# A two-block layer on one core: the gate tiles, the attention inputs and the convolution of the second block in another order

## The chip, the cores and the metric

The kernel runs on one NeuronCore of a Trainium2 chip. The metric is the time on the device in microseconds (us) for one execution, as a median over runs of the same program. Five engines with queues of their own take part: TensorE (PE in the rows, with its weight loads as PEld), VectorE (DVE), ScalarE (ACT), GpSimd (POOL), and SyncE (SP), which here only issues DMAs. Each engine works its queue in order: an instruction that waits holds up all that stands behind it on that engine.

## The reference, cut to what matters

`reference(...)` is a first block (a gated linear recurrence with a Fourier branch and expert-choice experts) and then `second_block`. Only the first half of the second block is touched here. With 512 tokens, 1024 channels, 8 heads of 64 and a convolution over 31 tokens it computes:

```python
proj = rmsnorm_2(x, norm_mix_g) @ w_in           # -> u_glu (1024), q, k, v (512 each), f_logit (8), gate_c, gate_a (1024 each)
a, gate = split(u_glu);  u = a * sigmoid(gate)   # 512 channels
u = causal_depthwise_conv(u, dw_w, 31 taps) + dw_b
conv_out = silu(layernorm(u, ln_g, ln_b)) @ pw_w            # -> 1024
c = cumsum(log_sigmoid(f_logit + fox_bf))                   # per head
s = (q @ k.T) * 64**-0.5 + c[query] - c[key]                # causal mask, softmax
attn_out = (softmax(s) @ v) @ attn_branch_w                 # -> 1024
merged = sigmoid(gate_c) * conv_out + sigmoid(gate_a) * attn_out
x = x + merged @ w_out                                      # then cross attention, experts, last norm
```

## The kernel before, in words

Every float32 matrix product is made of products of two parts: an operand is split into H (its rounded first part) and L (the rest), and three products (H·H, H·L, L·H) are summed; that is `mm3`, lines 87 to 90. A weight half of 128 rows by 512 comes from HBM as part of a 1 MB `raw` tile, ACT writes its H (`wH`, line 128) and GpSimd, or in places VectorE, its L (`wL`, line 129); four such pairs fit in the pool `wpc`. A projection tile of 128 output columns over 512 tokens (`ws_tile`) takes two halves, so 24 products; a tile with 512 input channels takes one half and 12 products. The `raw` tiles lie in four slots in this phase, and their loads stand in SP's queue.

The function touched is `phase_c`. Before the change it puts its work out in this order. The two norms between the blocks give the transposed input `hx` and write the normed rows back into `xres`, the residual (line 1246). Then come the gated linear unit, as two tiles of gates, two of values, and again (lines 1252 to 1263); the depthwise convolution on VectorE, 31 instructions for each of four channel tiles, from padded inputs `upad` into `cacc` (lines 1267 to 1277); the forget gates `fc` (lines 1281 to 1302); eight tiles of queries and keys and the values (lines 1305 to 1314); the layer norm over the channels with its `mean` and `var` products on TensorE (lines 1330 to 1354); and the attention, head by head.

`stack(p)` prepares a pair of heads. For each of the two it copies the first part of queries and keys into one half of the partitions of two tiles and the rest of the queries, and the first part of the keys once more, into the other half (ACT at lines 1370, 1371 and 1374, GpSimd at 1372 and 1373). These tiles take the four slots of the padded inputs: the first head's two tiles take the slots of the first two channel tiles of the convolution, which are free once the convolution has read them. `scores(h)` then makes three products for each of four blocks of queries: first parts with rests (1386), first part with the rest of the keys (1387), and the forget term through a selecting column (1388); the softmax runs on VectorE and ACT (1389 to 1396). `mix` transposes the weights `P`, copies them (`PT`, ACT or VectorE, lines 1408 and 1410), and multiplies with the values. Between two heads stand two steps named in the string `GC`: "G" is a gate tile of the convolution branch (24 products and a tanh), "C" a tile of its output product (12 products). After the last head the function `branch` makes for each of eight tiles the other gate (24 products) and the attention's output product (12).

What stands on a queue, and in which order, is decided by the framework's scheduler: it starts from the order in which the program emits its instructions and from what it thinks each takes, lets an instruction pass others when it believes it ready, and the result is fixed when the program is built. The order can be read without running; `tc.issue_after(i)` keeps what follows behind instruction `i`.

## Time and profile before

| what | value |
|---|---|
| median of 3 runs (lowest, highest) | 1777.76 us (1777.0, 1778.08) |
| span of the profiled execution, first to last instruction | 1772.1 us |
| median less that span | 5.7 us |
| mean granted TensorE clock | 0.969 of full speed |
| PE, PEld busy | 90 %, 59 % of the span |
| DVE, ACT, POOL busy | 49 %, 35 %, 30 % |
| HBM traffic over the span | 216 GB/s |

The profiled execution has no time of its own beside its span; the 5.7 us are what lies around the span, measured on other runs of the same program. Matmuls overlap in the records: one of 512 columns is on record for about 0.39 us and the next starts 0.23 us later, so counts in a window tell more than busy sums.

### The profile page before, as it was taken

What the parts mean: (1) busy time and instruction counts of PE and PEld (TensorE: products, weight loads), DVE (VectorE), ACT (ScalarE), POOL (GpSimd) and SP (SyncE); (2) the same over time, 40 slices, a digit from 0 to 9 for tenths busy, and PEclk for the clock granted to TensorE, in tenths of its full rate; (3) what the DMA queues carried; (4) which work ended last, traced back from release to release, by engine and by line L of the source; (5) the groups of instructions that cost most, each with busy time, mean ns of one, the idle gap of its engine ahead of it and who ended that gap; (6) DMA issues with size and microseconds to landing.
All of it is one profiled execution on the core that took longest, in us unless ns stands there. A gap on an engine that the chain in (4) does not pass through costs nothing. (4 is left out here: it accounts for less than half of the span.)

```text
span 1772.1 us, 20890 instructions
## 1 busy us (share of the span) xinstructions
PE 1597.7 (90%) x7766; PEld 1051.9 (59%) x7766; DVE 876.3 (49%) x1625; ACT 611.6 (35%) x1244; POOL 538.1 (30%) x431
## 2 busy tenths in 40 slices
PE   5988999999999999999999979779999988788884
PEld 4766677777775344434434347656667866666663
DVE  5388554333651221212122057996543264578886
ACT  3433355333430000000000152316533354478883
POOL 2213323344430000000000025745334442456654
PEclk9988999999999999999999989889999999889997
DMA  9423214454768999999999873111022229479934
GB/s 303 156 97 113 99 60 137 148 165 153 255 232 315 386 386 386 386 387 386 386 387 386 326 217 105 47 59 61 25 71 72 98 71 326 150 244 337 324 109 159
DMA packets 236076, 377.03 MB, mean 213 GB/s; under 512 B 16174, under 2 KB 107382, under 8 KB 235964
## 3 DMA queue, kind: packets, MB, share of 16 engines
q1 hardware_dynamic: 231644, 367.44, 58.7%
q0 software_dynamic: 4320, 8.16, 1.3%
q8 instruction: 63, 1.03, 0.2%
q14 instruction: 49, 0.40, 0.1%
HBM read 365.30 MB, written 17.83 MB: 216 GB/s over the span
## 5 line engine op out<-in xcount | busy, mean ns | idle before, releaser
L129 POOL TENSOR_TENSOR wL<-raw,wH 128x512 fp32r<-128x512 f32 x220 | 299.0, 1363 | 412.4 <-ACT wH L128 375.8
L128 ACT ACTIVATE wH<-raw 128x512 fp32r<-128x512 f32 x368 | 226.4, 629 | 276.3 <-PE ps L89 146.5
L1065 PE MATMUL ps<-raw,xT 128*64 128x512 f32 x512 | 228.1, 600 | 0.9 <-DMA raw<-in_w_up_e 0.9
L1066 PE MATMUL ps<-raw,xT 128*64 128x512 f32 x512 | 226.7, 600 | 1.6 <-DMA raw<-in_w_up_e 1.6
L1222 POOL TENSOR_TENSOR xg<-xres,raw 128x512 f32<-128x512 f32 x4 | 5.0, 1269 | 494.0 <-DVE xres L1122 494.0
L1066 PEld LDWEIGHTS ps<-raw,xT 128*64 128x64 f32 x512 | 69.4, 139 | 137.6 <-issue 132.6
L129 DVE TENSOR_TENSOR wL<-raw,wH 128x512 fp32r<-128x512 f32 x148 | 127.4, 906 | 28.5 <-ACT wH L128 26.9
L90 PE MATMUL ps<-raw,wL 128*128 128x512 f32 (+1 forms) x320 | 121.7, 380 | 9.7 <-POOL wL L129 9.7
L88 PE MATMUL ps<-raw,wH 128*128 128x512 f32 (+1 forms) x320 | 121.8, 381 | 0.0
L89 PE MATMUL ps<-raw,wH 128*128 128x512 f32 (+1 forms) x320 | 120.8, 378 | 0.0
L1107 DVE TENSOR_TENSOR hid<-hid,ps 128x512 f32<-128x512 f32 x16 | 11.0, 687 | 214.2 <-PE ps L1066 214.2
L1065 PE MATMUL ps<-raw,hidT 128*64 128x512 f32 x256 | 115.0, 596 | 0.0
L1106 ACT ACTIVATE hid<-ps 128x512 f32<-128x512 f32 x16 | 9.6, 597 | 303.7 <-PE ps L1066 303.7
L1066 PE MATMUL ps<-raw,hidT 128*64 128x512 f32 x256 | 113.5, 596 | 0.7 <-DMA raw<-in_w_down_e 0.7
L1276 DVE SCALAR_TENSOR_TENSOR cacc<-upad,dwc,cacc 128x512 f32<-128x512 f32 x120 | 109.1, 968 | 0.6
L88 PE MATMUL ps<-hx,wH 128*128 128x512 f32 x224 | 91.7, 409 | 3.3 <-ACT wH L128 3.3
L90 PE MATMUL ps<-hx,wL 128*128 128x512 f32 x224 | 90.8, 405 | 2.2 <-POOL wL L129 2.0
L89 PE MATMUL ps<-hx,wH 128*128 128x512 f32 x224 | 90.5, 404 | 0.0
L1826 POOL TENSOR_TENSOR dL<-raw,dH 128x512 fp32r<-128x512 f32 x64 | 82.3, 1307 | 21.8 <-ACT dH L1825 21.4
L1066 PEld LDWEIGHTS ps<-raw,hidT 128*64 128x64 f32 x256 | 33.7, 137 | 72.4 <-issue 69.3
L1065 PEld LDWEIGHTS ps<-raw,xT 128*64 128x64 f32 x512 | 69.3, 138 | 11.0 <-issue 8.9
L90 PEld LDWEIGHTS ps<-raw,wL 128*128 128x128 f32 x320 | 61.1, 191 | 23.5 <-POOL wL L129 10.2
(608 smaller groups left out, 3499.6 us busy)
## 6 DMA issues: line engine op xcount, KB each, us to landing
raw<-in_w_gate_e SPq DMA_DIRECT2D x64, 1024.0 KB
raw<-in_w_up_e SPq DMA_DIRECT2D x64, 1024.0 KB
raw<-in_w_down_e SPq DMA_DIRECT2D x64, 1024.0 KB
raw<-in_w_in SPq DMA_DIRECT2D x34, 1024.0 KB
raw<-in_w_ada SPq DMA_DIRECT2D x24, 1024.0 KB
raw<-in_expert_w_gate SPq DMA_DIRECT2D x32, 512.0 KB
raw<-in_expert_w_up SPq DMA_DIRECT2D x32, 512.0 KB
raw<-in_expert_w_down SPq DMA_DIRECT2D x16, 1024.0 KB
```

The source lines that it names most:

```text
L88: mm(ps, l[0], r[0], start=first, stop=False)
L89: mm(ps, l[0], r[1], start=False, stop=False)
L90: mm(ps, l[1], r[0], start=False, stop=last)
L128: self.nc.scalar.activation(out=H, in_=raw_ap, func=AF.Copy)
L129: (eng or self.lsub).tensor_tensor(out=L, in0=raw_ap, in1=H, op=OP.subtract)
L1065: nc.tensor.matmul(ps[0:64, :], act[:, k, 0:64], rA[:, q, :], start=k == 0, stop=k == 7, tile_position=(0, 0))
L1066: nc.tensor.matmul(ps[64:128, :], act[:, k, 64:128], rB[:, q, :], start=k == 0, stop=k == 7, tile_position=(0, 64))
L1106: AC.activation(out=hid, in_=pg, func=AF.Silu)
L1107: V.tensor_tensor(hid, hid, pu, op=OP.mult)
L1222: (nc.gpsimd, V)[XG[e][t]].tensor_tensor(out=xgs[t][e], in0=xs, in1=gf[:, e * 512:(e + 1) * 512], op=OP.mult)
L1276: V.scalar_tensor_tensor(acc, src, c, acc, op0=OP.mult, op1=OP.add)
L1826: (nc.gpsimd, V)[DL[i]].tensor_tensor(out=L, in0=src, in1=H, op=OP.subtract)
```

## The change

Five things change in `phase_c`. The loads for the gated linear unit are issued in pairs, and gate and value tile of the same channels follow one another, so that the convolution has its first input after two tiles rather than three; `gemm_ws2` takes its two tiles from two loads. The attention's gate (columns 3592 on) is no longer made in `branch`: its eight tiles become steps "A", and their tanh is kept in `xres`, whose rows are written to a DRAM tile `xrd` before and read back after. The layer norm becomes five steps "N". Seven gate tiles "G" now stand ahead of the attention (`FIRST`), and the rest of the steps between the heads (`BETWEEN`). `stack(h)` prepares one head; it also writes `qb` (the first part of the queries, with ones in the other half of the partitions) and `kb` (the rest of the keys, with the forget term in the other half), so that two products make a score and the third falls away; `stack(0)` and `stack(1)` are kept behind the last weight split of the seventh gate tile. Lines of comment are taken out all over the file, which moves the line numbers. The core of the diff:

```diff
-GC = "GGGGGCGCGCGCCCCC"
+FIRST = "GGGGGGG"
+BETWEEN = "NGA", "NNAA", "NNAA", "AC", "AC", "AC", "CC", "CCC"
...
-    def gemm_ws2(self, w, c0, act, evac, ct0=0):
...
+    def gemm_ws2(self, tiles, act):
+
+        W = [[self.wsplit(r[:, kk:kk + 4, q:q + 128], 4, 128, (self.nc.gpsimd, self.nc.vector)[E2[2 * j + kk // 4]]) for kk in (0, 4)]
+             for j, (r, q) in enumerate(tiles)]
         pss = [self.ps() for _ in W]
...
+        xrd = self.drp.tile([512, 1024], F32, name="xrd")
+        for t in range(4):
+            nc.sync.dma_start(out=xrd[t * 128:(t + 1) * 128, :], in_=xres[:, t, :])
+        tha = [xres[:, ct // 2, (ct % 2) * 512:(ct % 2 + 1) * 512] for ct in range(8)]
...
-             self.gemm_ws2(w, 512, hx, ev_gate))
-            self.gemm_ws(w, c2, 256, hx, ev_a, c2 // 128)
-
-        # ---- causal depthwise convolution
+            rg, ra = self.cols_chunk(w, 512 + c2, 8, 256), self.cols_chunk(w, c2, 8, 256)
+            for q in (0, 128):
+                ct = (c2 + q) // 128
+                pg, pa_ = (self.gemm_ws2([(rg, 0), (ra, 0)], hx) if ct == 0 else
+                           (self.ws_tile(rg, q, hx, 8), self.ws_tile(ra, q, hx, 8)))
+                ev_gate(ct, pg)
+                ev_a(ct, pa_)
+
...
+        def gate_steps(c0, new):
             for cc in range(0, 1024, 256):
-                r = self.cols_chunk(w, 2568 + cc, 8, 256)
+                r = self.cols_chunk(w, c0 + cc, 8, 256)
                 for q in (0, 128):
                     ct = (cc + q) // 128
...
+        def norm_steps():
+            ps = self.pa(name="mean")
+            for ct in range(4):
+                nc.tensor.matmul(ps, on, xc[ct], start=ct == 0, stop=ct == 3)
...
-                stacks[2 * p + a] = qa, ka, kl
+        def stack(h):
+
+            p, a = divmod(h, 2)
+            q, k = qk[p], qk[4 + p]
+            o, x = slice(64 * a, 64 * a + 64), slice(64 - 64 * a, 128 - 64 * a)
+            qb, kb = qb2[a], kb2[a]
+            qa, ka = (sa.tile([128, 544], F32, tag="upad", name="upad", bufs=NST)[:, 0:512].bitcast(F32R) for _ in range(2))
+            AC.activation(out=qa[o], in_=q[o], func=AF.Copy)
+            AC.activation(out=ka[o], in_=k[o], func=AF.Copy)
+            nc.gpsimd.tensor_tensor(out=qa[x], in0=q[o], in1=qa[o], op=OP.subtract)
+            nc.gpsimd.tensor_tensor(out=kb[o], in0=k[o], in1=ka[o], op=OP.subtract)
+            AC.activation(out=ka[x], in_=ka[o], func=AF.Copy)
+            AC.activation(out=qb[o], in_=q[o], func=AF.Copy)
+            c = x.start + h
+            AC.activation(out=kb[x], in_=cf[x].bitcast(F32), func=AF.Copy, scale=self.selR[x, c:c + 1].bitcast(F32))
+            stacks[h] = qa, ka, qb, kb
 
         def scores(h):
-            """the weights of the keys, queries on the partitions."""
-            qa, ka, kl = stacks.pop(h)
-            r = 64 * (h % 2)
...
                 n = 128 * (i + 1)
                 s = self.pa(name="s")
                 b = slice(i * 128, (i + 1) * 128)
                 nc.tensor.matmul(s[:, 0:n], qa[:, b], ka[:, 0:n], start=True, stop=False)
-                nc.tensor.matmul(s[:, 0:n], qa[r:r + 64, b], kl[r:r + 64, 0:n], start=False, stop=False)
-                nc.tensor.matmul(s[:, 0:n], self.selR[r:r + 40, r + h:r + h + 1].to_broadcast([40, 128]), cf[r:r + 40, 0:n], start=False, stop=True)
+                nc.tensor.matmul(s[:, 0:n], qb[:, b], kb[:, 0:n], start=False, stop=True)
...
+        steps = {"G": gate_steps(2568, new_thc), "A": gate_steps(3592, lambda ct: tha[ct]), "C": conv_steps(), "N": norm_steps()}
+
+        def run(names):
+            for x in names:
+                next(steps[x])
+        run(FIRST)
+        wH, wL = self.split_ins
+        with tc.issue_after(wH), tc.issue_after(wL):
+            stack(0)
+            stack(1)
         nxt = scores(0)
...
             P = nxt
-            if h in (0, 2, 4):
-                stack(h // 2 + 1)
             if h < 7:
                 nxt = scores(h + 1)
-            for x in GC[2 * h:2 * h + 2]:
-                next(gates if x == "G" else convs)
+            if h < 6:
+                stack(h + 2)
+            run(BETWEEN[h])
             if h % 2 == 0:
                 po = self.pa(name="po")
...
+            wr = self.raw(I["attn_branch_w_2"][0][:, cc:cc + 512].rearrange("(k p) c -> p k c", p=128), 4, 512)
+            for c2 in range(0, 512, 128):
+                ct = (cc + c2) // 128
+                py = self.ws_tile(wr, c2, aS, 4)
+                th = tw(name="gth")
+                V.scalar_tensor_tensor(th, tha[ct], 1.0, py, op0=OP.add, op1=OP.mult)
+                V.tensor_tensor(th, thc[ct], th, op=OP.add)
+                H, L = self.split(th, HL("m"), 0.5)
+                mS[0].append(H)
+                mS[1].append(L)
+        for t in range(4):
+            nc.sync.dma_start(out=xres[:, t, :], in_=xrd[t * 128:(t + 1) * 128, :])
+
```

Where instructions move, the order of the queues shows it at three places.

ACT, at the first `stack`, before; `upad` are the stacked heads in the slots of the padded inputs, `qk2` the evacuated queries and keys, `wH` the first parts of weights (the values' weights follow below these rows):

```order
L1309 ACTIVATE qk2_7318<-ps_7285 128x512
L1309 ACTIVATE qk2_7353<-ps_7320 128x512
L1309 ACTIVATE qk2_7390<-ps_7357 128x512
L1370 ACTIVATE upad_7782<-qk2_7318 64x512
L1309 ACTIVATE qk2_7425<-ps_7392 128x512
L128 ACTIVATE wH_7481<-raw_7427 128x512
L1371 ACTIVATE upad_7783<-qk2_7390 64x512
L1374 ACTIVATE upad_7783<-upad_7783 64x512
L128 ACTIVATE wH_7502<-raw_7499 128x512
L128 ACTIVATE wH_7518<-raw_7499 128x512
L1309 ACTIVATE qk2_7462<-ps_7429 128x512
L128 ACTIVATE wH_7537<-raw_7499 128x512
```

ACT, at the first `stack`, after; `thc` are the gates of the convolution branch:

```order
L1333 ACTIVATE thc_7839<-ps_7840 128x512
L129 ACTIVATE wH_7950<-raw_7946 128x512
L129 ACTIVATE wH_7966<-raw_7946 128x512
L1333 ACTIVATE thc_7876<-ps_7877 128x512
L1388 ACTIVATE upad_7983<-qk2_7323 64x512
L1389 ACTIVATE upad_7984<-qk2_7395 64x512
L1393 ACTIVATE qb0_7724<-qk2_7323 64x512
L1392 ACTIVATE upad_7984<-upad_7984 64x512
L1395 ACTIVATE kb0_7726<-fc_7275,selR_229 64x512
L1388 ACTIVATE upad_7992<-qk2_7323 64x512
L1389 ACTIVATE upad_7993<-qk2_7395 64x512
L1393 ACTIVATE qb1_7725<-qk2_7323 64x512
```

The first stack stood among the queries' and keys' projections, ahead of `wH_7502` and of all weight splits behind it; now it stands behind the splits of the seventh gate tile.

PE, at the first score, before; `var` is the norm's variance, `ps` are projection tiles, `s` the scores, `kl` the rest of the keys:

```order
L88 MATMUL ps<-raw,wH 128x512
L1340 MATMUL var<-csq,on_7715 128x512 x4
L1386 MATMUL s<-upad 128x128
L1387 MATMUL s<-kl,upad 128x128
L1388 MATMUL s<-fc,selR 128x128
L1386 MATMUL s<-upad 128x256
L1387 MATMUL s<-kl,upad 128x256
L1388 MATMUL s<-fc,selR 128x256
```

PE, at the norm's `mean`, after; these are the scores of head 1, and `ps` is the eighth gate tile:

```order
L89 MATMUL ps<-raw,wH 128x512
L1406 MATMUL s<-upad 128x384
L1407 MATMUL s<-kb_7727,qb_7725 128x384
L90 MATMUL ps<-raw,wH 128x512
L1406 MATMUL s<-upad 128x512
L1407 MATMUL s<-kb_7727,qb_7725 128x512
L91 MATMUL ps<-raw,wL 128x512
L89 MATMUL ps<-raw,wH 128x512
L1348 MATMUL mean<-cacc,on_7720 128x512 x4
L90 MATMUL ps<-raw,wH 128x512
```

The variance stood right ahead of the first score, seven projection products behind the mean. Now the scores of heads 0 and 1 stand ahead of the mean, seven projection products apart, nine more projection products follow the mean, and then comes the variance; a score has two products where it had three.

DVE, at the norm's reciprocal, before; `crv` is the variance, then its reciprocal root:

```order
L1342 TENSOR_SCALAR crv<-var 128x512
L1389 TENSOR_TENSOR s<-s,mask_n 128x128 x2
L1391 TENSOR_REDUCE am<-s 128x1 x2
L1392 TENSOR_SCALAR am<-am 128x1
L1389 TENSOR_TENSOR s<-s,mask_n 128x128
L1392 TENSOR_SCALAR am<-am 128x1
L1389 TENSOR_TENSOR s<-s,mask_n 128x128
L1391 TENSOR_REDUCE am<-s 128x1
L1344 RECIPROCAL crv<-crv 128x512
L1392 TENSOR_SCALAR am<-am 128x1
L1391 TENSOR_REDUCE am<-s 128x1
L1347 TENSOR_TENSOR cacc<-cacc,crv 128x512 x2
```

DVE, at the same place after; `PT` are the transposed weights of head 0:

```order
L1415 TENSOR_SCALAR P<-P,am 128x512
L1351 TENSOR_TENSOR cacc<-cacc,mean 128x512 x4
L1356 TENSOR_SCALAR crv<-var 128x512
L1358 RECIPROCAL crv<-crv 128x512
L1429 COPY PT<-pt 128x512
L1361 TENSOR_TENSOR cacc<-cacc,crv 128x512 x2
L1362 TENSOR_SCALAR cacc<-cacc,cols_889 128x512 x2
L1429 COPY PT<-pt 128x256
L1361 TENSOR_TENSOR cacc<-cacc,crv 128x512 x2
L1362 TENSOR_SCALAR cacc<-cacc,cols_889 128x512
L1408 TENSOR_TENSOR s<-s,mask_n 128x128 x2
L1410 TENSOR_REDUCE am<-s 128x1 x2
```

The reciprocal stood among the first softmax; now the softmax of two heads stands ahead of the norm, and the copies `PT` of head 0, which its product with the values needs, stand behind the reciprocal and behind four more of the norm's instructions.

## Rows read from the trace of the kernel before

**Rows 1.** Busy time by stage: engine busy us (instructions), granted clock, DMA share, GB/s

```profile
1135.00:1155.00 20.00, 10.27 (x35) 7.89 (x34) 19.87 (x23) 4.52 (x8) 19.92 (x7) 0.74 0.17 52
1155.00:1175.00 20.00, 20.00 (x88) 16.16 (x87) 20.00 (x22) 4.13 (x7) 8.89 (x6) 1.00 0.33 106
1175.00:1195.00 20.00, 8.48 (x28) 6.10 (x27) 19.79 (x25) 2.30 (x4) 7.02 (x4) 0.66 0.03 4
1225.00:1340.00 115.00, 114.93 (x485) 75.63 (x486) 57.80 (x182) 53.66 (x132) 41.31 (x32) 1.00 0.14 46
1340.00:1420.00 80.00, 80.00 (x345) 64.35 (x344) 24.43 (x25) 25.85 (x45) 36.28 (x28) 1.00 0.28 99
```

**Rows 2.** PE waits, 1055 to 1440 us: total us, times, longest

```profile
PE ps L90 <- POOL wL L129: 9.7, 1, 9.7
PE ps L88 <- ACT wH L128: 9.1, 1, 9.1
PE ps L89 <- POOL wL L129: 3.0, 2, 2.4
PE s L1386 <- ACT P L1394: 1.1, 1, 1.1
```

**Rows 3.** Timeline of ACT: start us, length us, [idle before, its releaser]

```profile
1130.53 0.62 ACT L128 ACTIVATE wH<-raw 128x512 fp32r<-128x512 f32 x1
1142.36 0.63 ACT L1371 ACTIVATE upad<-qk 64x512 fp32r<-64x512 f32 x1 [11.21 <-DVE cacc L1276]
1185.41 0.63 ACT L1370 ACTIVATE upad<-qk 64x512 fp32r<-64x512 f32 x1 [18.22 <-DVE cacc L1276]
```

**Rows 4.** Timeline of POOL in the same stretch

```profile
1130.29 15.88 POOL L1372 TENSOR_TENSOR upad<-qk,upad 64x512 fp32r<-64x512 f32 x1 [1.61 <-ACT upad L1370]
1186.18 2.05 POOL L1372 TENSOR_TENSOR upad<-qk,upad 64x512 fp32r<-64x512 f32 x1 [17.25 <-ACT upad L1370]
```

**Rows 5.** POOL by line, 1055 to 1195: count, busy us, mean ns

```profile
L129 POOL TENSOR_TENSOR wL<-raw,wH 128x512 fp32r<-128x512 f32 x36 | 55.9, 1558 | 40.9 <-ACT wH L128 40.4
```

**Rows 6.** Timeline of DVE: start and end of the causal convolution

```profile
1073.31 0.69 DVE L1259 SCALAR_TENSOR_TENSOR upad<-glu,ps 128x512 f32<-128x512 f32 x1 [11.24 <-PE ps L90]
...
1197.80 0.49 DVE L1277 TENSOR_SCALAR cacc<-cacc,cols 128x512 f32<-128x512 f32 x1
```

**Rows 7.** Timeline of PE: the narrowest and widest third score product, with their successors

```profile
1239.59 0.27 PE L1388 MATMUL s<-fc,selR 40*128 40x128 f32 x1
1239.79 0.39 PE L1386 MATMUL s<-upad 128*128 128x256 f32 x1
...
1243.39 0.39 PE L1388 MATMUL s<-fc,selR 40*128 40x512 f32 x1
1243.70 0.50 PE L90 MATMUL ps<-raw,wL 128*128 128x512 f32 x1
```

**Rows 8.** Groups by line, 1200 to 1340 us

```profile
L1391 DVE TENSOR_REDUCE am<-s 128x1 f32<-128x128 f32 (+3 forms) x32 | 14.9, 484 | 0.2
L1396 DVE TENSOR_SCALAR P<-P,am 128x128 f32<-128x128 f32 (+3 forms) x32 | 14.8, 482 | 0.3
L1389 DVE TENSOR_TENSOR s<-s,mask_n 128x128 f32<-128x128 f32 x32 | 9.5, 297 | 21.6 <-PE s L1388 21.3
L1334 PE MATMUL mean<-cacc,on 128*128 128x512 f32 x8 | 3.6, 592 | 0.0
L1347 DVE TENSOR_TENSOR cacc<-cacc,crv 128x512 f32<-128x512 f32 x4 | 3.7, 953 | 0.0
L1344 DVE RECIPROCAL crv<-crv 128x512 f32<-128x512 f32 x1 | 3.3, 3341 | 0.0
```

**Rows 9.** Groups by line, 1340 to 1420 us

```profile
L1448 DVE TENSOR_TENSOR gth<-thc,gth 128x512 f32<-128x512 f32 x8 | 12.7, 1587 | 0.3
L192 DVE SCALAR_TENSOR_TENSOR mL<-gth,mH 128x512 fp32r<-128x512 f32 x8 | 5.5, 692 | 5.6 <-ACT mH L191 5.6
L1447 DVE SCALAR_TENSOR_TENSOR gth<-gth,ps 128x512 f32<-128x512 f32 x8 | 5.5, 688 | 39.3 <-PE ps L90 39.3
```

More of the change, by code (lines that the diff above doesn't have):

```diff
@@ L1327, in gate_steps, with new_thc @@
                     yield
+        def new_thc(ct):
+            thc[ct] = tp(name="thc")
+            return thc[ct]
         on = sa.tile([128, 128], F32, tag="on128", name="on128", bufs=1)
         V.memset(on, 1.0 / 512.0)
-        ps = self.pa(name="mean")
-        for ct in range(4):
-            nc.tensor.matmul(ps, on, xc[ct], start=ct == 0, stop=ct == 3)
-        psv = self.pa(name="var")
-        for ct in range(4):
-            V.tensor_tensor(xc[ct], xc[ct], ps, op=OP.subtract)
-            sq = tw(name="csq")
-            AC.activation(out=sq, in_=xc[ct], func=AF.Square)
-            nc.tensor.matmul(psv, on, sq, start=ct == 0, stop=ct == 3)
@@ L1341, in phase_c @@
-        rv = tw(name="crv")
-        V.tensor_scalar(rv, psv, EPS, None, op0=OP.add)
-        AC.activation(out=rv, in_=rv, func=AF.Sqrt)
-        V.reciprocal(rv, rv)
-        cS = [], []
-        for ct in range(4):
-            V.tensor_tensor(xc[ct], xc[ct], rv, op=OP.mult)
-            V.tensor_scalar(xc[ct], xc[ct], self.ln_g[:, ct:ct + 1], self.ln_b[:, ct:ct + 1], op0=OP.mult, op1=OP.add)
-            th = tw(name="cth")
-            AC.activation(out=th, in_=xc[ct], func=AF.Tanh, scale=0.5)
-            V.scalar_tensor_tensor(xc[ct], th, 1.0, xc[ct], op0=OP.add, op1=OP.mult)
-            H, L = self.split(xc[ct], HL("c"), 0.5)
-            cS[0].append(H)
-            cS[1].append(L)
+        cS = [], []
@@ new lines, in norm_steps @@
+        def norm_steps():
+            ps = self.pa(name="mean")
+            for ct in range(4):
+                nc.tensor.matmul(ps, on, xc[ct], start=ct == 0, stop=ct == 3)
+            psv = self.pa(name="var")
+            for ct in range(4):
+                V.tensor_tensor(xc[ct], xc[ct], ps, op=OP.subtract)
+                sq = tw(name="csq")
+                AC.activation(out=sq, in_=xc[ct], func=AF.Square)
+                nc.tensor.matmul(psv, on, sq, start=ct == 0, stop=ct == 3)
+            rv = tw(name="crv")
+            V.tensor_scalar(rv, psv, EPS, None, op0=OP.add)
+            AC.activation(out=rv, in_=rv, func=AF.Sqrt)
+            V.reciprocal(rv, rv)
+            yield
+            for ct in range(4):
+                V.tensor_tensor(xc[ct], xc[ct], rv, op=OP.mult)
+                V.tensor_scalar(xc[ct], xc[ct], self.ln_g[:, ct:ct + 1], self.ln_b[:, ct:ct + 1], op0=OP.mult, op1=OP.add)
+                th = tw(name="cth")
+                AC.activation(out=th, in_=xc[ct], func=AF.Tanh, scale=0.5)
+                V.scalar_tensor_tensor(xc[ct], th, 1.0, xc[ct], op0=OP.add, op1=OP.mult)
+                H, L = self.split(xc[ct], HL("c"), 0.5)
+                cS[0].append(H)
+                cS[1].append(L)
+                yield
@@ L1421, in conv_steps @@
                     yield
-        gates, convs = gate_steps(), conv_steps()
-        stack(0)
+        steps = {"G": gate_steps(2568, new_thc), "A": gate_steps(3592, lambda ct: tha[ct]), "C": conv_steps(), "N": norm_steps()}
[7 more added lines that the diff above has]
+            stack(1)
         nxt = scores(0)
@@ L1444, in phase_c @@
         mS = [], []
-        def ev_at(ct, th, py):
-            V.scalar_tensor_tensor(th, th, 1.0, py, op0=OP.add, op1=OP.mult)
-            V.tensor_tensor(th, thc[ct], th, op=OP.add)
-            H, L = self.split(th, HL("m"), 0.5)
-            mS[0].append(H)
-            mS[1].append(L)
-        self.branch(I["attn_branch_w_2"][0], w, 3592, aS, hx, lambda: tw(name="gth"), ev_at)
+        for cc in range(0, 1024, 512):
+            wr = self.raw(I["attn_branch_w_2"][0][:, cc:cc + 512].rearrange("(k p) c -> p k c", p=128), 4, 512)
[10 more added lines that the diff above has]
+            nc.sync.dma_start(out=xres[:, t, :], in_=xrd[t * 128:(t + 1) * 128, :])
         self.gemm_ta(I["w_out_2"][0], 0, mS, 8, 4, ev_res(0))
```

36 lines of the change are left out of this document (12 added, 24 removed).

## The prediction, made before the changed kernel was run

> **What bounds the kernel now.** I read the page first: PE is busy for 90 % of the span and no other engine for more than 60 %, and in the slices of time from 1107 to 1196 us its share falls to seven tenths. The busy time by stage shows what the whole-span shares hide [rows 1]. From 1155 to 1175 us PE starts 88 matmuls in 20 us at full clock, so one per 0.227 us; from 1225 to 1340 us it is busy for 114.93 of 115 us and from 1340 to 1420 us for 80 of 80. In these stretches TensorE's own work is the time, and moving work about inside them gains nothing. From 1135 to 1155 us it starts 35, at a mean granted clock of 0.74, and from 1175 to 1195 us 28, at 0.66. There something else is the bound.
>
> The waits say what [rows 2]: one idle time of 9.7 us until a weight rest from POOL, one of 9.1 us until a first part from ACT, 3.0 us in two more until POOL, and 1.1 us at a score. The timelines of ACT and POOL show what stood ahead of these. ACT made a split at 1130.53 us and then sat for 11.2 us at an instruction of the first `stack` until the convolution let go of a slot, and later for 18.2 us at another, until 1185.41 us [rows 3]. POOL's part of the same stack began at 1130.29 us and is on record for 15.88 us [rows 4]. The convolution on VectorE gets its first input at 1073.31 us and ends at 1198.3 us, 125.0 us without a gap that counts [rows 6]. So the bound of this stage is neither PE nor VectorE by itself, but weight splits that stand on ACT's and POOL's queues behind stacks that need the convolution's slots.
>
> **The change, part by part.** All of it is summed against the profiled span of 1772.1 us; the median of the runs is 5.7 us longer, and I carry these 5.7 us over unchanged.
>
> *The stacks move behind the seventh gate tile.* The two places lose 88 − 35 = 53 and 88 − 28 = 60 matmuls, which at 0.227 us is 12.0 and 13.6 us [rows 1]. Of these 25.7 us, 21.8 are the three idle sums of [rows 2], and 3.9 the clock after each: the mean grants of 0.74 and 0.66 say that part of each stretch ran at the lower of the two levels (1.2 in place of 2.4 GHz), after PE had stood still, while the stretch between shows 1.00. Both go if nothing else is late there. What is late next? PE comes to the split of the seventh gate tile, two tiles ahead of its product, 23 tiles of 24 products after 1073.31 us: 23 x 24 x 0.227 = 125 us, near 1199 us. The convolution now starts one tile (5.5 us) sooner and so ends near 1193 us. That leaves 6 us, and behind it the four split pairs that ACT and POOL are ahead (four times 12 products, 10.9 us), of which the eleven stack instructions of 0.63 us [rows 3] eat 6.9. A convolution that is 8 us late costs nothing. POOL's ordinary splits during the convolution took 1.56 us each on the mean of 36 [rows 5], and PE needs one per 2.7 us. Value: −25.7.
>
> *The third score product goes.* 32 matmuls. From its start to the next start passes 0.20 us in the narrowest block and 0.31 us in the widest [rows 7]; at the mean, 0.255, that is 8.2 us. PE was busy around the heads, so this counts in full. The second product now has 128 rows in place of 64; I take its time as unchanged, since the projection products, with 128 rows, start 0.227 us apart at 512 columns [rows 1], no more than the 0.31 us of the third product with its 40 rows at that width [rows 7]. Value: −8.2. The price is two more ACT copies a head, 16 x 0.63 = 10 us on an engine that was busy for 53.66 of 115 us [rows 1]; hidden as long as ACT is not asked for something else at once.
>
> *Gate tiles and attention gates move.* Seven tiles come ahead of the attention and eight attention gates from behind it into it; the count of products is the same. Value 0. The 1.1 us wait of [rows 2] goes with its place (−1.1), but the place gets new ones.
>
> *The norm moves into the first heads.* From the first score to the variance PE has 16 score products, 25 projection products and the mean: 41 x 0.237 (115 us over 485 records, [rows 1]) and 3.6 us [rows 8], together 13.3 us. By the new order VectorE does both softmaxes ahead of the norm's subtractions. Masks, maxima and scalings are 39.2 us for eight heads [rows 8], so 9.8 us for two; the whole VectorE time of 57.8 us over the seven heads of that stage [rows 1] bounds it from above with 16.5 us. Then four subtractions of about 0.69 us (the same form as in [rows 9]) alternate with squares on ACT, which has both further stacks ahead of them. So the variance waits between 0 and 4.5 us. I take 2.5, nearer the upper end, since the small instructions are left out of the lower. Next, the reciprocal takes 3.34 us and four more norm instructions at 0.95 us [rows 8] stand between two copies of head 0's transposed weights, while PE has only some 2 us of work between them: 0 to 3.8, I take 1.5. For the other heads, 0 to 3, taken as 1.5: their filler is as long as before, and before they cost 0.07 us. Value of the three: +5.5, between 0 and 11.3.
>
> *The branch without its gate tiles.* A tile now has 12 products, 2.7 us, and VectorE needs 23.7 us for eight [rows 9], 2.96 us each; so it falls behind by 1.9 us in all, and the first product after the heads has no gate tile in front of it. The next projection hides most. Value +1, between 0 and 3.
>
> *The residual's way through DRAM.* Three of the four writes, which wait for ACT's last scaled rows, stand on SP ahead of the second gate load, which PE needs four tiles (21.8 us) after its first product. At the rate of [rows 1] (106 GB/s at a share of 0.33, so about 320 at a full share) 2 MB of writes and this load are 10 us. The way back is four loads for which SP waits on VectorE; two further loads of the output projection stand behind them, the first of which is wanted only after 96 products, 22 us later. Cover in both cases; 0, and up to 4 us where the load is late.
>
> Sum: −25.7 − 8.2 − 1.1 + 5.5 + 1.0 = −28.5. Span 1743.6, and with the 5.7 us a time of 1749 us.
>
> **The rivals.** *No new waits.* Everything but the +6.5 holds: 1743 us. For it speaks that PE lost 0.07 us over seven heads before [rows 1]; against it the new order, which puts 13 us of VectorE work ahead of the variance.
>
> *Splits still wait for VectorE.* POOL's 15.88 us [rows 4] is no ordinary duration: the same instruction took 2.05 us at the next stack, also during the convolution. ACT's wait does not explain it, since its input was there. If POOL can be held off by a running convolution in that way, an ordinary split can be too, and PE, now at full rate, asks for splits over all of the convolution. The price of one such case is that of the first stall as it stands, 12.0 us [rows 1]: 1761 us. Against it speak the 36 ordinary splits with their mean of 1.56 us [rows 5]. The Trainium skill bears on this (SBUF — State Buffer, "Who interferes with whom"): a VectorE instruction with both inputs in SBUF contends with GpSimd's reads, and the one that comes second is blocked for the whole instruction. By that rule a split would wait for one convolution instruction at a time, which the mean of 1.56 us would contain, and the sum stays; the 15.88 us is longer than any one instruction, so the rule alone does not cover it.
>
> *Slower.* The norm in the first three heads leaves PE idle as long as the stacks did. It decides from where VectorE's share of a head (up to 8.3 us, 57.8 over seven, and two norm steps with some 6 us) passes PE's cycle (48 products of filler, 11 us, and some 6 us of the head itself). That is 14 against 17 us, so it would have to be 3 us worse than I make it, in each of three heads, with an idle time that costs the clock as well. At the 12.8 us that a stall cost on the mean [rows 1], three of them are 38.5 in place of my 5.5: 1782 us.
>
> *Nothing comes of it.* The gain is given back in small waits all through the heads: 1777 us.
>
> **How the numbers follow.** Chances: forecast 0.70, no new waits 0.14, splits still waiting 0.10, nothing 0.02, slower 0.04. A measurement of this kernel tells about 0.2 %, 3.6 us, from no change. The first three cases are faster, so 0.94; same 0.02; slower 0.04. The bounds of the unknown terms, added up, reach from 1743 to about 1757; the range goes to 1740 at the low end, for products that start closer together than 0.227 us, and to 1762 at the high end, to hold the case of one held-off split.
>
> **What would show it.** In the changed profile PE should stand at 87 or 88 matmuls and a granted clock of 1.00 in every 20 us from 1075 to about 1205 us, and ACT's waits for `cacc` should be gone: that is the first term. The score's third product has no rows, and a head's scores take about 1 us less: the second. Waits of PE at the variance product for ACT's squares, and at the product with the values for a VectorE copy, of some 1 to 4 us each, show the third; none of them shows the rival with 1743. A wait for a split on POOL before 1193 us, or a granted clock below 1 in that stretch, shows the other rival. The forecast is wrong if PE waits for more than some 12 us in all between the first score and the output projection, or if the output projection waits for its residual rows.

## The result: 1737.2 us, faster than forecast and below the range

The changed kernel takes 1737.18 us in the median (1734.41 to 1738.66, 4 runs) against 1777.65 us of the kernel before, a ratio of 0.9775 (95 % interval 0.9761 to 0.9789). The forecast was 1749 us, the range 1740 to 1762. The direction was right, the gain of 40.5 us is 12 us larger than forecast. In two later series of runs the changed kernel took 1736.83 and 1738.16 us, and the kernel before had medians between 1773.7 and 1777 us.

Where it came from is best seen between two marks on TensorE that both kernels have: the first transpose of the norm between the blocks and the last transpose of the next norm. One row per kernel, of the instructions of one line (min/median/max ns, then first and last start). Before:

```profile
L1209 PE MATMUL pa<-ident,hn x64: 270/273/477, 1046.0 to 1461.8; 128*128 128x128 f32 x64
```

After:

```profile
L1209 PE MATMUL pa<-ident,hn x64: 271/273/475, 1048.3 to 1430.3; 128*128 128x128 f32 x64
```

| profiled runs | to the first mark | between the marks | from the last mark to the end | span |
|---|---|---|---|---|
| before; its second profile | 1046.0; 1050.1 | 415.8; 416.5 | 310.3; 308.1 | 1772.1; 1774.7 |
| after; two more profiles | 1048.3; 1049.1; 1051.7 | 382.0; 381.6; 383.4 | 303.6; 303.5; 304.9 | 1733.9; 1734.2; 1740.0 |

The stretch between the marks is what the change touches, and it repeats within 2 us. It lost 33.8 us (415.8 − 382.0), where the forecast's sum was 28.5. Another 6.7 us of the first pair of profiles lie behind it, in code that is the same.

The windows that answer to [rows 1] in the changed kernel (busy us of PE, PEld, DVE, ACT and POOL with instructions, granted clock, DMA share, GB/s):

```profile
1135.00:1155.00 20.00, 17.06 (x67) 13.38 (x67) 19.87 (x24) 4.62 (x8) 19.24 (x6) 0.91 0.30 85
1155.00:1175.00 20.00, 20.00 (x88) 16.20 (x87) 20.00 (x20) 4.92 (x8) 10.63 (x7) 1.00 0.34 102
1175.00:1195.00 20.00, 20.00 (x88) 16.23 (x87) 19.96 (x20) 9.65 (x15) 10.24 (x7) 1.00 0.26 78
1225.00:1340.00 115.00, 113.58 (x488) 78.23 (x489) 66.62 (x190) 67.95 (x152) 44.44 (x35) 1.00 0.17 55
```

The second stall is gone (28 matmuls are 88 now). Of the first, 35 became 67, at a granted clock of 0.91 where 1.00 is the upper of the two levels: 21 matmuls or 4.8 us are still lost there. Its waits from 1065 to 1400 us, to be read beside [rows 2]:

```profile
PE ps L91 <- POOL wL L130: 2.9, 1, 2.9
PE ps L89 <- DVE gth L1477: 1.7, 1, 1.7
PE ps L90 <- DVE cL L192: 0.8, 1, 0.8
PE s L1406 <- ACT P L1413: 0.6, 1, 0.6
PE var L1354 <- ACT csq L1353: 0.2, 1, 0.2
```

The first row is what is left in the place of the old stall: a weight rest that PE needs is late on POOL. The timelines of POOL and VectorE in that place:

```profile
1137.42 11.15 POOL L130 TENSOR_TENSOR wL<-raw,wH 128x512 fp32r<-128x512 f32 x1 [0.32 <-ACT wH L129]
```

```profile
1137.30 8.02 DVE L1285 SCALAR_TENSOR_TENSOR cacc<-upad,dwc,cacc 128x512 f32<-128x512 f32 x12
...
1147.37 2.90 DVE L1310 CAST fc<-fe 8x512 fp32r<-8x512 f32 x2
```

One ordinary split took 11.15 us, where their mean was 1.56 [rows 5]. Meanwhile VectorE ran convolution instructions 0.66 us apart (12 in 8.02 us), and POOL's instruction ended 1.2 us after the forget gates' first cast had begun. The 15.88 us of [rows 4] is the same event in the kernel before, there on a stack's instruction: VectorE's convolution instructions lie 0.66 us apart beside it too. Both come again in every further profile of the two kernels (15.88 us; 11.14 and 11.17 us).

The scores, to be read beside [rows 7], one group of them on PE's timeline:

```profile
1219.97 0.34 PE L1406 MATMUL s<-upad 128*128 128x384 f32 x1
1220.14 0.34 PE L1407 MATMUL s<-kb,qb 128*128 128x384 f32 x1
1220.32 0.39 PE L1406 MATMUL s<-upad 128*128 128x512 f32 x1
1220.55 0.40 PE L1407 MATMUL s<-kb,qb 128*128 128x512 f32 x1
1220.79 0.39 PE L89 MATMUL ps<-raw,wH 128*128 128x512 f32 x1
```

The two products of the widest block take 0.47 us from the first start to the projection's start (1220.79 − 1220.32). Added up over the records, from each score product's start to the next start on PE, the scores took 26.6 us for 96 products before and 12.1 us for 64 after: 0.277 and 0.190 us each. So 14.5 us went, where the forecast had 8.2. By kind, the third products took 8.1 us before, about what the forecast had; the other 64 products took 18.5 us before and 12.1 after, and these 6.4 us were not in the forecast.

### The profile page after: what moved, and what is told of

The parts are those of the page before. It is cut to its first block, busy times and chain, and to the rows that moved or that the text cites. A ratio compares the mean times of both kernels' runs of the same rounds, so it can differ in the third digit from the quotient of the medians.

```text
span 1733.9 us, 20855 instructions
## 1 busy us (share of the span) xinstructions
PE 1580.3 (91%) x7734; PEld 1044.1 (60%) x7734; DVE 881.7 (51%) x1625; ACT 622.5 (36%) x1261; POOL 536.7 (31%) x433
## 5 line engine op out<-in xcount | busy, mean ns | idle before, releaser
L130 POOL TENSOR_TENSOR wL<-raw,wH 128x512 fp32r<-128x512 f32 x220 | 311.9, 1423 | 421.3 <-ACT wH L129 393.0
L1285 DVE SCALAR_TENSOR_TENSOR cacc<-upad,dwc,cacc 128x512 f32<-128x512 f32 x120 | 117.8, 1034 | 0.9
L1120 PE MATMUL pa<-y,PT 128*128 128x512 f32 x128 | 59.2, 605 | 12.3 <-DVE y L1117 12.3
```

What stands on the lines that cost most here:

```text
L130: j = (eng or self.lsub).tensor_tensor(out=L, in0=raw_ap, in1=H, op=OP.subtract)
L1120: nc.tensor.matmul(ps, PT[:, t * 128:(t + 1) * 128], y, start=True, stop=True)
L1285: V.scalar_tensor_tensor(acc, src, c, acc, op0=OP.mult, op1=OP.add)
```

## Experiments

In the profiles, "stretch" is the time between the two marks above; times are medians, with the ratio to the kernel before and its interval.

**What made the scores cheaper.** Four edits of the changed kernel's score products, nothing else. They are for times alone: the second run counts the rests and the forget term twice, the third leaves the forget term out, the fourth also the rests of the queries.

```diff
 nc.tensor.matmul(s[:, 0:n], qa[:, b], ka[:, 0:n], start=True, stop=False)
-nc.tensor.matmul(s[:, 0:n], qb[:, b], kb[:, 0:n], start=False, stop=True)
# first run: the three products of before
+nc.tensor.matmul(s[:, 0:n], qa[r:r + 64, b], kb[r:r + 64, 0:n], start=False, stop=False)
+nc.tensor.matmul(s[:, 0:n], self.selR[r:r + 40, ...], cf[r:r + 40, 0:n], start=False, stop=True)
# second run: the 128-row product twice
+nc.tensor.matmul(s[:, 0:n], qb[:, b], kb[:, 0:n], start=False, stop=False)
+nc.tensor.matmul(s[:, 0:n], qb[:, b], kb[:, 0:n], start=False, stop=True)
# third run: the second product on 64 rows; fourth run: the first on ka[r:r + 64] as well
+nc.tensor.matmul(s[:, 0:n], qa[r:r + 64, b], kb[r:r + 64, 0:n], start=False, stop=True)
```

> The changed kernel, with the three score products of the kernel before in place of its two: the second on 64 rows, the third on the 40 rows of the forget term. All copies of the changed kernel stay. Theory of the forecast: the second product costs the same on 64 rows as on 128, and the third costs 8.2 us, so 1737.2 + 8.2 = 1745 us. Rival (a product whose number of rows differs from that of the product in front of it starts about 0.1 us late): the whole difference of the score groups comes back, 26.6 - 12.1 = 14.5 us, so 1752 us.

> The changed kernel with a third score product of 128 rows (the second once more, so rests and forget terms count twice). Theory of the forecast: a third product costs 0.255 us whatever its rows, 8.2 us, 1745 us. Rival (rows): with all products on 128 rows it costs what the two cost now, 12.1 us / 64 = 0.19 us each, 6.1 us, 1743 us; far under the 14.5 us that three products of 128, 64 and 40 rows would add.

> The changed kernel, with its second score product on the 64 rows of the head alone (the forget term is left out of the scores). The number of products is unchanged. Theory of the forecast: rows don't matter, 1737 us. Rival (rows): the 64-row product and the product behind it start about 0.1 us late each, 64 times, so +6 us, 1743 us.

> The changed kernel, with both score products on the 64 rows of the head (rests of the queries and the forget term are left out of the scores), for the distance from one start to the next. Theory (a change of the number of rows from one product to the next costs): 64 rows behind 64 rows start as close as 128 behind 128, 0.25 us at 512 columns, and only the products at the ends of a group are late, so the scores take between 13 and 17 us. Rival (fewer rows cost by themselves): every product starts 0.1 us or more later, some 21 us as in the run with one of 64 rows.

| products of a block (rows) | scores, all heads | stretch | median (ratio, interval) |
|---|---|---|---|
| 128, 128 (changed kernel) | 12.1 us, 64 x 0.190 | 382.0 | 1737.18 |
| 128, 64, 40 | 26.6 us, 96 x 0.277 | 398.2 | 1751.26 (0.9884, 0.9846 to 0.9921) |
| 128, 128, 128 | 17.4 us, 96 x 0.181 | 388.0 | 1746.09 (0.9854, 0.9812 to 0.9896) |
| 128, 64 | 20.8 us, 64 x 0.326 | 390.9 | 1745.26 (0.9854, 0.9816 to 0.9891) |
| 64, 64 | 14.3 us, 64 x 0.223 | 387.6 | 1743.94 (one run) |

Undoing the layout brings all 14.5 us of the scores back (the stretch is 16.2 us longer), and a third product of 128 rows only 5.2. With 64 rows after 128, two products cost more than three of 128. Rows of the third run's timeline, in the block of 384 columns and the block of 512:

```profile
1299.99 0.44 PE L1406 MATMUL s<-upad 128*128 128x384 f32 x1
1300.36 0.44 PE L1408 MATMUL s<-kb,upad 64*128 64x384 f32 x1
1300.73 0.50 PE L91 MATMUL ps<-raw,wL 128*128 128x512 f32 x1
...
1302.23 0.39 PE L1406 MATMUL s<-upad 128*128 128x512 f32 x1
1302.55 0.49 PE L1408 MATMUL s<-kb,upad 64*128 64x512 f32 x1
```

At 384 columns each of the two starts is followed by the next after 0.37 us, against 0.17 and 0.18 in the changed kernel. In the fourth run, inside a group of blocks, 64 rows follow 64 rows:

```profile
1299.78 0.39 PE L1407 MATMUL s<-upad 64*128 64x256 f32 x1
1300.00 0.28 PE L1408 MATMUL s<-kb,upad 64*128 64x256 f32 x1
1300.13 0.34 PE L1407 MATMUL s<-upad 64*128 64x384 f32 x1
1300.31 0.33 PE L1408 MATMUL s<-kb,upad 64*128 64x384 f32 x1
1300.57 0.50 PE L91 MATMUL ps<-raw,wL 128*128 128x512 f32 x1
1300.91 0.39 PE L89 MATMUL ps<-raw,wH 128*128 128x512 f32 x1
```

There they start 0.13 to 0.22 us apart, as 128 rows do (in the blocks of 512 columns, most of them right behind a projection, it is 0.32 on the mean, where 128 rows have 0.27); the gap to the projection, where the rows change back, is 0.26, and the projection's own next start is 0.34 us away in place of 0.23. So it is the change of rows, not their number, that costs 0.1 to 0.2 us at a product. From 64 to 40 rows it is less, up to 0.1 us (0.28 us at 384 columns in the kernel before, 0.18 from 64 to 64). The sum of the fourth run lies in the 13 to 17 us of that theory. It leaves out the projections beside a group: of the 5.6 us that the stretch is longer, the scores have 2.1 and the projection products, waits included, 3.3. The Trainium skill (TensorEngine Tiling (Array Packing), "Key Properties") says that changing the tiling mode drains TensorE; it gives no price, and the rows agree that a change costs time. Whether the products wait for such a drain or for their weight loads, the rows do not show.

**What the place of the stacks was worth.**

```diff
+        stack(0)
+        stack(1)
         run(FIRST)
-        wH, wL = self.split_ins
-        with tc.issue_after(wH), tc.issue_after(wL):
-            stack(0)
-            stack(1)
```

> The changed kernel, with the stacks of the first two heads issued ahead of the seven gate tiles and not kept behind their splits, so that their copies stand among the queries' and keys' projections again. Theory of the forecast: both stalls come back, +25.7 us, 1763 us, with ACT waiting for the convolution and PE for splits. Rival one (a held-off POOL, not the place of the stacks, made the first of the two stalls, and the changed kernel still pays some 4.8 us of it): +20 us, 1757 us. Rival two (the gain came from the scores and elsewhere, and the stall is hidden by the other order): under +8 us.

1760.62 us (0.9928, 0.9907 to 0.9948); the stretch is 407.8 us, 25.8 longer, so the forecast's theory holds. PE's longest waits between the marks, ACT's waits in the stacks, and POOL's part of the first stack:

```profile
PE ps L89 <- ACT qk L1318: 13.6, 1, 13.6
PE ps L89 <- ACT wH L129: 6.9, 1, 6.9
PE ps L91 <- POOL wL L130: 3.5, 2, 2.8
```

```profile
ACT upad L1389 <- DVE cacc L1285: 17.6, 2, 14.4
ACT upad L1388 <- DVE cacc L1285: 16.2, 1, 16.2
```

```profile
1126.88 1.62 POOL L1390 TENSOR_TENSOR upad<-qk,upad 64x512 fp32r<-64x512 f32 x1 [0.74 <-ACT upad L1388]
```

POOL was not held off here (1.62 us) and PE still stood for 13.6 us: ACT's wait for the convolution's slots is enough for the stall by itself. That 25.8 is so near the forecast's 25.7 is partly chance. The stalls of this run cost more: 29, 56 and 46 matmuls in the three windows of 20 us from 1135 us, where 88 fit, are 133 lost, or 30.2 us; but the 4.8 us that the changed kernel loses at POOL are not among them.

**The norm's place.**

```diff
-FIRST = "GGGGGGG"
-BETWEEN = "NGA", "NNAA", "NNAA", "AC", "AC", "AC", "CC", "CCC"
+FIRST = "GGGGGGGN"
+BETWEEN = "GA", "AA", "AA", "AC", "AC", "AC", "CC", "CCC"
...
         run(FIRST)
+        run("NNNN")
```

> The changed kernel, with all five steps of the norm issued ahead of the stacks and scores, and not in the first three heads. Theory of the forecast: the norm in the first heads costs 5.5 us, so without it 1732 us. Rival (the trace of the changed kernel shows only 0.2 us of waiting at the variance and 0.8 us at the branch's first parts): nothing to gain, 1737 us, and slower if the stacks and first scores now wait for the norm, by up to 13 us (VectorE's work of two softmaxes and ACT's stacks no longer lie beside the gate tiles).

1737.47 us (0.979, 0.9767 to 0.9812), stretch 383.8. The rival was right: the norm in the first heads costs nothing that its other place would save (there PE waits 0.9 and 1.8 us for copies of the weights).

**What lies outside.** Both kernels once more.

> The kernel before itself, for a second profile. If the 5.7 us lie around the span, as the forecast took it, time less span is 5.7 us again. Rival: 1.9 us lie around the span and the profiled run of before was 3.8 us under the median. Also: the stretch from the last transpose of the next norm to the end was 310 us in before and 304 us after. If that belongs to the change, it is 310 us again; if the 3.92 us of one VectorE instruction in the router (0.17 us after) is an accident of the moment, it may be some 306 us as well.

> The changed kernel itself, as the base for the other runs of this call and for a second profile: 1737 us, between 1734 and 1741 us. In its profile the stretch from the first transpose of the norm between the blocks to the last one of the next norm should be 382 us again, where it was 415.8 us before.

> The changed kernel once more, as the base of this call: 1737 us, between 1731 and 1739 us.

The changed kernel took 1736.83 us (0.9777, 0.9754 to 0.9801) and 1738.16 us (0.979, 0.9768 to 0.9811), as expected. Time less span was 1.9 us for the kernel before (1776.62 and 1774.7), as in every run of this study that shows both (1.7 to 1.9). The 5.7 us of the table of before were therefore 1.9 us around the span and 3.8 us by which the profiled run was quicker than the median. Behind the last mark the second profile of before has 308.1 us. In both profiles of before one VectorE instruction of the router took 3.9 us; VectorE and POOL there, in the first of them:

```profile
1538.06 0.65 DVE L1663 CAST tri<-s 128x128 fp32r<-128x128 f32 x1 [1.30 <-DMA s<-in_tri]
1538.63 3.92 DVE L1682 TENSOR_SCALAR s<-s 128x8 f32<-128x8 f32 x1
```

```profile
1537.36 2.49 POOL L1610 TENSOR_TENSOR hm<-xres,raw 128x512 f32<-128x512 f32 x2
1539.79 2.73 POOL L1769 MEMSET xsb<- 128x1024 f32 x3
```

And VectorE after:

```profile
1505.32 0.22 DVE L1696 CAST tri<-s 128x128 fp32r<-128x128 f32 x1
1505.45 0.17 DVE L1715 TENSOR_SCALAR s<-s 128x8 f32<-128x8 f32 x1
```

VectorE came behind a late DMA into a train of POOL instructions and was done when that ended (1542.5 us); after, it came before the train. The run with three products of 128 rows had the late DMA and the 3.92 us too, and 306.4 us behind the mark; all others of the changed kernel's kind have 302 to 305. So some 3.7 of the 6.7 us (3.92 − 0.17) hang on a load's landing, not on work that was saved. The other 3 us were not traced.

**What holds POOL off.** The forget gates' chain stood at the beginning and the end of the 11.15 us, so it was tried first: ACT instead of VectorE for the scaling and the casts, then the whole chain earlier.

```diff
-            V.tensor_scalar(e_, e_, -8.0, None, op0=OP.mult)
...
-                V.tensor_copy(cf[r:r + 8], e_)
-                V.tensor_tensor(cf[r + 32:r + 40], e_, cf[r:r + 8], op=OP.subtract)
+                AC.activation(out=cf[r:r + 8], in_=e_, func=AF.Copy, scale=-8.0)
+                V.scalar_tensor_tensor(cf[r + 32:r + 40], e_, -8.0, cf[r:r + 8], op0=OP.mult, op1=OP.subtract)
# second run: the chain as it was, in the loop of the gated linear unit
                 ev_a(ct, pa_)
+                if ct == 0:
+                    bf = sm.tile([8, 1], F32, tag="bf", name="bf", bufs=1)
...
```

> The changed kernel, with VectorE's scaling by -8 and its two casts of the forget gates given to ACT (the subtraction takes the scale). Theory: POOL's one weight rest of 11.15 us (its others take about 1.5 us), during which TensorE lost some 4.8 us, begins at VectorE's TENSOR_SCALAR on 8 partitions and ends at its cast, so without the two POOL is not held off and the time is some 4 to 5 us less, 1733 us. Rival one: the unbroken alternation of two convolution tiles alone holds POOL off, and the long weight rest stays: 1737 us. Rival two: ACT now waits for VectorE's scan with weight splits behind it, so up to 3 us more: 1740 us.

> The changed kernel, with the forget gates' product and VectorE's work on them right behind the first pair of tiles of the gated linear unit, where a single tile of the convolution runs, and not behind all four pairs. Theory (POOL is held off while two convolution tiles alternate on VectorE behind the forget gates' scan): the weight rest of 11.15 us is gone, the 4.8 us of TensorE between 1135 and 1155 us come back, 1732 us. Rival one (the hold-off follows the forget gates wherever they stand): the long weight rest moves to some 1085 us, and the time stays 1737 us or rises as far as 1745 us, since fewer splits are in store there. Rival two (any long stretch of alternating tiles does it): the long rest stays near 1140 us, 1737 us.

The first took 1743.24 us (0.9813, 0.9794 to 0.9832): the long rest stays, 10.51 us, and PE waits 9.0 us for it, since ACT stood 6.1 us before its casts and its splits came late; both rivals happened at once. The second took 1767.29 us (0.9951, 0.9934 to 0.9968), beyond all that was expected. POOL in that run, and PE's wait for it:

```profile
1134.01 34.77 POOL L130 TENSOR_TENSOR wL<-raw,wH 128x512 fp32r<-128x512 f32 x1 [8.19 <-ACT wH L129]
```

```profile
PE ps L91 <- POOL wL L130: 25.1, 1, 25.1
```

So the forget gates do not hold POOL off. In the changed kernel the hold-off ended at their casts; in the run with the early chain it ended where a single tile of the convolution was left and VectorE's next start came 0.77 us after the last, not 0.66 (1166.91 and 1167.68 us). What VectorE does in all these stretches is two tiles of the convolution in turn, so that no instruction needs the one ahead of it: each takes 0.73 us and they start 0.66 us apart. The next runs put the tiles one after the other (`tc.issue_after` on the last instruction of the tile ahead), then with more gate tiles ahead of the stacks, since the convolution ends later that way (1221 in place of 1208 us); one is a control without the order tile by tile, and one lets the last two tiles alternate again.

```diff
+            with ExitStack() as hold:
+                if prev is not None:          # last run: and ct < 3
+                    hold.enter_context(tc.issue_after(prev))
...
-FIRST = "GGGGGGG"
-BETWEEN = "NGA", "NNAA", "NNAA", "AC", "AC", "AC", "CC", "CCC"
# second and third run
+FIRST = "GGGGGGGG"
+BETWEEN = "NAA", "NNAA", "NNAA", "AC", "AC", "CC", "CC", "CC"
# fourth and fifth run
+FIRST = "GGGGGGGGA"
+BETWEEN = "NA", "NNAA", "NNAA", "AC", "AC", "CC", "CC", "CC"
```

> The changed kernel, with the convolution's four tiles one after the other on VectorE and not two in turn, so that each instruction needs the one ahead of it. Theory (POOL comes in only where VectorE's instructions leave a gap, and two tiles in turn, 0.663 us from start to start at 0.733 us each, leave none): no weight rest on POOL above 5 us before the scores, the 4.8 us of TensorE come back, 1733 us; the convolution ends later, by some 0.1 us per instruction that was in turn, up to 12 us, near the first stack, which may take part of it back. Rival (it is the moment at which POOL's instruction starts that counts, or the work of the forget gates): a long weight rest stays or moves, 1737 us or more.

> The convolution's tiles one after the other, as in the run before, and an eighth gate tile ahead of the stacks (one attention gate goes from the second half of the heads into the first filler in its place). Theory (the one loss that the order tile by tile brought is ACT's 6.7 us, where the stacks ask for the convolution's end some 14 us later than in the changed kernel): one gate tile, 24 products or 5.5 us, covers most of it, POOL is not held off, and the time is 1732 to 1736 us, at or under the changed kernel's 1737 us. Rival: the shorter fillers of the last heads leave waits, and nothing is gained: 1739 us or more.

> The changed kernel with that eighth gate tile alone, two tiles of the convolution in turn as in the changed kernel. POOL's 11 us weight rest should be there again (it stands 60 us ahead of the moved tile). Theory (the stacks had cover enough already): 1737 us. Rival (the shorter fillers of the last heads cost): 1739 to 1742 us.

> The convolution tile by tile as in the two runs of that kind, with eight gate tiles and one attention gate ahead of the stacks. Theory (what is left of the stall is the 3.1 us behind the stacks and the clock after it): with one more tile of 24 products, 5.5 us, nothing waits for the convolution any more, the stretch between the two norms' transposes falls from 382 to some 378 us and the time to 1733 us. Rival (the time goes elsewhere in the heads, whose fillers get shorter): 382 us or more in that stretch, 1737 us.

> The same, but only the first three tiles of the convolution one after the other; the third and the fourth alternate again, from some 1155 us on. Theory (an unbroken alternation is what holds POOL off): a weight rest on POOL of 10 us or more appears between 1155 and 1200 us, PE waits for it, and the time is 5 to 25 us longer than that of the run tile by tile. Rival (only the stretch around the forget gates holds POOL off): no such rest, the convolution ends earlier, and the time is the same or better.

| run | longest weight rest, 1060 to 1240 us | convolution ends | stretch | median (ratio, interval) |
|---|---|---|---|---|
| changed kernel | 11.15 us | 1208 | 382.0 | 1737.18 |
| tile by tile | 2.46 | 1221 | 389.2 | 1742.72 (0.9815, 0.9787 to 0.9844) |
| and one gate tile more ahead | 2.43 | 1219 | 384.9 | 1737.83 (0.9789, 0.9776 to 0.9802) |
| that gate tile alone | 11.14 | 1209 | 382.4 | 1737.80 (0.9784, 0.9771 to 0.9798) |
| tile by tile, two tiles more ahead | 2.43 | 1227 | 381.8 | 1735.33 (0.9777, 0.9760 to 0.9793) |
| three tiles in order, the last two in turn | 2.54 | 1216 | 378.1 | 1731.75 (0.9762, 0.9746 to 0.9777) |

Tile by tile the long rests are gone, and the stall comes back at the stacks, as ACT's 6.7 us of the first of these runs show:

```profile
PE ps L89 <- ACT wH L129: 6.7, 1, 6.7
```

The second and the third of these runs differ in the order alone: the longest rest is 2.43 us with it and 11.14 without, but the time is the same, and with the order PE waits 3.1 us for ACT near the stacks. The fourth run was expected at a stretch of 378 us and got 381.8; PE has short waits there that the last run lacks, 3.1 us in all. In the last run nothing is left of either; its windows:

```profile
1135.00:1155.00 20.00, 20.00 (x88) 16.22 (x87) 19.62 (x21) 6.37 (x11) 12.36 (x8) 1.00 0.35 105
1155.00:1175.00 20.00, 20.00 (x88) 16.22 (x87) 20.00 (x20) 5.09 (x9) 11.06 (x8) 1.00 0.35 106
1175.00:1195.00 20.00, 20.00 (x87) 16.12 (x86) 20.00 (x19) 8.91 (x14) 11.57 (x8) 1.00 0.36 106
```

Its stretch is 3.9 us shorter than the changed kernel's, and its median the lowest of the study, by some 5 us against the changed kernel's in other series; the intervals of the two ratios overlap. It also says that the theory was too simple: the last two tiles alternate from 1155 us on and POOL was not held off, as that run's rival had it. But the rival's own cause, the forget gates, does not fit the 34.77 us. Over all profiles of this study there are 24 POOL instructions with VectorE's next three starts 0.66 us apart from the outset and inside them, and these 24 took 2.7 to 34.8 us (beside the two of 15.88 us that began some 2 us later). Fifteen of them came after POOL had waited some 7.6 us or more, the nine of 11.1 us behind the forget gates' scaling. Where POOL has a split every few VectorE instructions the two take turns, at 1.5 us a split. What decides which of the two rhythms sets in was not settled.

## Why the prediction was wrong in its size

| term | forecast | measured | by |
|---|---|---|---|
| stacks behind the seventh gate tile | −25.7 | −20.9 | windows: 21 of the 113 matmuls lost before are still lost |
| third score product | −8.2 | −14.5 | starts on PE, and the run that undoes it |
| score wait | −1.1 | −0.5 | 0.6 us left |
| norm in the first heads | +5.5 | +1.0 | waits of 0.2 and 0.8 us; norm first gains nothing |
| branch without gate tiles | +1.0 | +1.7 | wait for `gth` |
| between the marks | −28.5 | −33.2 of 33.8 | |
| outside the marks | 0 | −4.4 | +2.3 before the first, −6.7 behind the last |

The step that failed is in the second term: "The second product now has 128 rows in place of 64; I take its time as unchanged". The comparison behind it was of projection products of 128 rows with the third product of 40, 0.227 against 0.31 us [rows 7], and was read as harmless. It held the answer: the 0.31 us is what a product costs beside products with other rows. All three products of a block paid that, not only the one that went: the third product itself was sized rightly (8.1 us), but the other two, taken as unchanged, fell from 18.5 to 12.1 us, so the term was worth 14.5 us. With it at that size the forecast would have been 1743 us. The Trainium skill's rule on tiling modes (TensorEngine Tiling (Array Packing), "Key Properties": a change drains TensorE) was not weighed in the prediction, and it spoke for a larger gain.

The first term's mechanism was right, and the run that undoes it gives 25.8 us, though that number is partly chance. One reading in it was wrong and changes no sum: of the 3.0 us until POOL in [rows 2] only 2.4 belong to the stall, and 0.6 lie near 1438 us, so the clock's share was 4.4 us and not 3.9. But the rival "Splits still wait for VectorE" also happened: the hold-off moved from a stack's instruction to a split. Its price was put at a whole stall, 12.0 us, and was 4.8: PE went on for some 8 us after POOL's instruction had begun, with splits in store, and waited 2.9. The forecast asked for a weight rest late on POOL as the sign, and that is the 2.9 us of the waits.

The norm's term was too pessimistic. VectorE's timeline, from the first mask of head 0 to the norm's subtractions:

```profile
1219.88 0.59 DVE L1408 TENSOR_TENSOR s<-s,mask_n 128x128 f32<-128x128 f32 x2 [11.81 <-PE s L1407]
...
1231.71 2.48 DVE L1351 TENSOR_TENSOR cacc<-cacc,mean 128x512 f32<-128x512 f32 x4
```

The softmax of two heads took 11.8 us, inside the range taken, and PE's own work up to the variance covered it but for 0.2 us. (The upper bound of 4.5 us there does not come out of its terms: 16.5 + 4 x 0.69 − 13.3 is 6.0.) The copies of the weights were never waited for.

The convolution did not end near 1193 us but at 1208. The forecast carried its 125 us over, but it took 138 us (1070.0 to 1208.1): where VectorE started 22 and 25 instructions in 20 us from 1155 us on before [rows 1], it now started 20, while POOL had 7 in each window in place of 6 and 4. That is more than the 8 us that were worked out as free, but TensorE was late itself by 2.3 us at the first mark and 4.8 us at POOL, and ACT reached the first stack at 1209.4 us and did not wait.

The bounds of the terms between the marks led to a low end of 1743 us, and the 3 us below it were left for closer starts; nothing was left for the rest of the span, which gave 4.4 us in the profiled pair, and the 5.7 us carried over were not all outside the span (the changed kernel's median lies 3.3 us above its profiled span).

## What to carry to other kernels

A matmul is priced from its start to the next start and together with its neighbours: a narrow product among full ones costs them too, so making all products of a group the same shape can be worth nearly as much (6.4 us here) as dropping one (8.1 us). Where VectorE runs long rows of instructions that don't need one another, look at what POOL has to deliver meanwhile; an order in which each instruction needs the one ahead can be the cheaper one, if what waits for the row's end has other work to cover it. Profile the kernel before twice before a difference outside the edited stage is put down to the edit.

## What was not expected of the hardware

- A change of the number of rows between matmuls (128 to 64 or back, 40 to 128) costs 0.1 to 0.2 us at the products around it, from 64 to 40 up to 0.1 us; 64 rows after 64 rows, inside a group, start as close as 128 after 128.
- A POOL instruction of some 1.5 us took 10.5, 11.15, 15.88 and 34.77 us beside VectorE instructions that started 0.66 us apart and overlapped. The Trainium skill's rule (SBUF — State Buffer, "Who interferes with whom"), one instruction at a time, does not cover that. The reverse was seen too: VectorE's 3.92 us behind POOL's two products and three memsets.
